# Four of the eight blocks of two feed-forward column groups as seven products of two by two blocks, with the sums formed in float32

## The chip, the cores and the metric

The kernel runs on one core of one Trainium2 chip. The metric is the device time of one execution, in microseconds (us). The core has a matmul engine (TensorE, in the profile PE with its weight loads PEld), a vector engine (DVE), a scalar engine (ACT), GpSimd (POOL) and a queue that starts transfers (SP). Matmuls write to eight PSUM banks of 128 x 512 float32; DVE and ACT read the banks, POOL does not.

## The reference, cut to what matters

Two layers of a decoder trunk on 256 tokens of width 1024, each with three gated token mixers and a feed-forward part. The change is in the feed-forward part of each layer:

```python
h2 = _rms_norm(x, ffn_norm)
x = x + (jax.nn.silu(h2 @ w_ffn_gate) * (h2 @ w_ffn_up)) @ w_ffn_down
```

Here h2 is 256 x 1024 and gate and up are 1024 x 2816 each. All is float32 and has to come out at float32's accuracy or close to it.

## The kernel before, in words

**Products.** TensorE multiplies numbers of a shorter format (F32R). So every operand is split in two, `hi` (rounded by ACT, `hi_of`, L223) and `lo` (what is left, a subtraction on DVE, `lo_of`, L226), and a product is three matmuls: hi by hi, hi by lo, lo by hi.

**Weights.** `weight_plan` (L51) cuts every weight into pieces of 128 x 1024 numbers at most, in the order of their use; for the feed-forward's first layer a piece is two blocks of 128 rows of the contraction by 512 columns. `dma_piece` (L241) loads a piece on SP's queue into one of five `raw` tiles. `split_piece` (L268) splits it into one of five pairs `whi`, `wlo` and then starts the load of the piece that takes the freed raw tile. `take` (L277) is called for each piece that is to be multiplied; it first splits the piece three further on.

**First layer of the feed-forward.** `ffn` (L1002) goes over the columns in groups of 1024: 512 of gate, then the same 512 of up, five such groups and a last one of half the size, for both layers. Gate and up take one `rows_job` (L297) each. It has one bank for each half of the 256 rows (b = 0, 1) and goes over the eight contraction blocks k in four pieces; for each k and each b it issues three matmuls with 512 columns, so 12 for a piece, 48 for a job and 96 for a group. The inputs are the normalised rows, `xs[k]`, as hi and lo:

```python
self.mm(ps[b], h, wh, k == 0, False)
self.mm(ps[b], h, wl, False, False)
self.mm(ps[b], lo, wh, False, k == nk - 1)
```

After gate's job ACT takes tanh of each bank (L1008) and DVE forms the gate from it (L1009); after up's job DVE multiplies it in (`product`, L1012). The rows so made are transposed by TensorE (`transposed`, L465, eight matmuls for a group), and split for the second layer, in `hidden_pairs` (L994), which is called after the second piece of the next group.

**Before it.** `out_proj` (L975) ends the mixers. It adds its two halves of columns to the rows x (`x_tm`, L989), and in its second half it calls `norm_pairs((0, 1))` (L473): TensorE transposes the first half of x into a bank, ACT writes gain times the bank as hi (L224) and DVE what is left as lo (L231). Pairs 2 and 3 follow in the feed-forward's first job. ACT also squares x for the norm (L413).

**Order.** The kernel is written as a stream of operations in program order. The framework then sets a fixed order for each engine, by its own estimate of when an operation is ready, and adds the waits; so an operation may stand ahead of one that was written before it. PSUM is two rings of four banks, `bank` for weight products and `att` for transposes and attention. `fr` is a ring of 18 pairs of tiles for split operands, `f` one of nine float32 tiles.

Of the kernel before, what the change touches and what calls it, by code (L numbers as in the profile page):

```python
# [12 lines left out]
F32 = mybir.dt.float32  # L13
# [35 lines left out]


def weight_plan():  # L51
    plan = []

    def block(name, l, nk, c0, ncols):
        per = max(1, PIECE // ncols)
        for k in range(0, nk, per):
            plan.append((name, l, k, min(per, nk - k), c0, ncols))

    def mixer_in(l, off):
        for c in range(0, 1024, 256):  # L60
            block("w_in", l, KT, off + c, 256)

    for l in range(DEPTH):
        block("w_in", l, KT, OFF_C, N_C)
        mixer_in(l, OFF_AQ)
        block("mla_w_uq", l, 3, 0, 768)
        block("mla_w_ukv", l, 2, 0, 1024)
        block("w_in", l, KT, OFF_AV, 512)
        mixer_in(l, OFF_BQ)
# [7 lines left out]
        for n in range(2 * FF // 512):  # L77
            block("w_ffn", l, KT, n * 512, 512)
# [5 lines left out]
    return plan  # L84


BRANCHES = ((0, "w_branch_a"), (2, "w_branch_c"), (1, "w_branch_b"))
PLAN = weight_plan()


def shape_constants():
# [84 lines left out]
def fields(t):  # L176
    v = t.rearrange("p (c f t) -> p c f t", c=2, f=2)
    return v[:, :, 0], v[:, :, 1]
# [6 lines left out]
class Build:  # L185
    def __init__(self, nc, tc, ctx, x, xt, w, lam, fnorm, cst, out):
        self.nc, self.tc = nc, tc
        self.x_in, self.xt_in, self.w_in = x, xt, w
        self.lam_in, self.fnorm_in, self.cst_in, self.out = lam, fnorm, cst, out
        self.cp = cp = ctx.enter_context(tc.tile_pool(name="cp", bufs=1))  # L190
        pp = ctx.enter_context(tc.tile_pool(name="pp", bufs=1, space=PSUM))

        def ring(n, cols, dt, name, pool=cp):
            return Ring([pool.tile([128, cols], dt, name=f"{name}{i}") for i in range(n)])

        self.banks = ring(N_DENSE, 512, F32, "bank", pp)
# [7 lines left out]
        self.raw = [cp.tile([128, PIECE], F32, name=f"raw{i}") for i in range(N_RAW)]  # L204
# [31 lines left out]
    def split(self, hi, lo, src, scale=None):  # L236
        self.hi_of(hi, src, 1.0 if scale is None else scale)
        self.lo_of(lo, src, hi, scale)


    def dma_piece(self, queue=None):  # L241
        if self.n_dma < len(PLAN):
# [3 lines left out]
            (queue or self.nc.sync).dma_start(out=self.raw[self.n_dma % N_RAW][:, :n], in_=src)  # L246
            self.woff += 128 * n
            self.n_dma += 1

    def first_split(self):  # L250

        hi, lo, raw = self.whi[0], self.wlo[0], self.raw[0]
# [10 lines left out]
        self.n_split = 1  # L263
        self.dma_piece()
        self.xg.append(t)
        self.xs += chunks([t])

    def split_piece(self):  # L268
        i = self.n_split
        if i < len(PLAN):  # L270
            n = PLAN[i][3] * PLAN[i][5]
            j = i % N_PIECE
            self.split(self.whi[j][:, :n], self.wlo[j][:, :n], self.raw[i % N_RAW][:, :n])
            self.n_split += 1
            self.dma_piece()

    def take(self):  # L277
        self.split_piece()
        i = self.taken
        self.taken += 1  # L280
        _, _, _, nk, _, nc_ = PLAN[i]
# [29 lines left out]
    def setup(self):  # L311
# [10 lines left out]
        for p in range(1, 4):  # L322
            nc.sync.dma_start(out=self.x0[p], in_=self.x_in[:, G_W + 512 * p:G_W + 512 * p + 512])
            self.dma_piece()
        self.ones = cp.tile([128, 128], F32, name="ones")
        nc.vector.memset(self.ones, 1.0)  # L326
        self.ones_r = cp.tile([128, 128], F32R, name="ones_r")
# [11 lines left out]
        self.vc = [cp.tile([128, 8, 2, 64], F32R, name=f"vc{b}") for b in range(2)]  # L339
        self.q_tm = cp.tile([128, 2, 8, 96], F32, name="q_tm")  # L340
        self.k_tm = cp.tile([128, 2, 8, 96], F32, name="k_tm")
# [131 lines left out]
    def norm_pairs(self, pairs, g0):  # L473
        for p in pairs:
            bank, ps = self.transposed(self.x_tm, p * 256)
            self.split_pair(p, ps, g0)
            self.att.put(bank)


    def dense(self, l):  # L480
# [491 lines left out]
            pump(2 if s < SLOW else 1)  # L972


    def out_proj(self, pairs, nk, g0, late):  # L975
        self.fresh_norm()
        self.ss = [self.small(), self.small()]
        for n in range(2):
            bank = [self.banks.get() for _ in range(2)]
            for i, _ in enumerate(self.rows_job(bank, ChunkList(pairs), nk)):  # L980
                if n == 0 and i == 0:
                    late()
                if n == 1 and i == 1:
                    self.norm_pairs((0, 1), g0)
# [17 lines left out]
    def ffn(self):  # L1002
# [8 lines left out]
        def product(b, a, u):  # L1011
            nc.vector.scalar_tensor_tensor(out=a, in0=a, scalar=self.rr[:, b:b + 1], in1=u, op0=ALU.mult, op1=ALU.mult)  # L1012

        for i in range(5):
            a = [self.f.get() for _ in range(2)]
            bank = [self.banks.get() for _ in range(2)]
            for j, _ in enumerate(self.rows_job(bank, self.xs, KT)):
                yield
                if j == 1 and self.waiting:
                    self.hidden_pairs(*self.waiting)  # L1020
            for b in range(2):
                gated(b, a[b], bank[b])
            self.banks.put(*bank)
# [84 lines left out]
    def run(self):  # L1108
        self.n_norm = 0
        self.setup()  # L1110
        for l in range(DEPTH):
# [30 lines left out]
            self.attention(l, pump)  # L1142
            for _ in stream:
                pass
            self.out_proj(self.mp, KT, G_FFN + 8 * l, lambda: self.mixed(1))
            stream = self.ffn()
            pump(1)
            self.norm_pairs((2, 3), G_FFN + 8 * l)
# [6 lines left out]
        assert self.taken == len(PLAN)  # L1155


def pack_weights(arrs):
# [40 lines left out]
```

## Time and profile before

| | |
|---|---|
| Time, median of 3 runs | 880.74 us (880.54 to 880.96) |
| Profiled execution, its own time | 880.81 us |
| Its span, first to last instruction | 879.0 us |
| PE busy, and PEld | 871.7 us (99%), 755.8 us (86%) |
| DVE busy | 591.7 us (67%) |
| ACT busy | 503.0 us (57%) |
| POOL busy | 55.5 us (6%) |
| DMA | 155.90 MB, mean 177 GB/s |

Busy is the share of the span in which an engine had an instruction under way. Matmuls are pipelined, so PE's busy time overlaps from one matmul to the next, and the mean duration of one is longer than the step from one to the next.

### The profile page before, as it was taken

What the parts mean: (1) busy time and instruction counts of PE and PEld (TensorE: products, weight loads), DVE (VectorE), ACT (ScalarE), POOL (GpSimd) and SP (SyncE); (2) the same over time, 40 slices, a digit from 0 to 9 for tenths busy, and PEclk for the clock granted to TensorE, in tenths of its full rate; (3) what the DMA queues carried; (4) which work ended last, traced back from release to release, by engine and by line L of the source; (5) the groups of instructions that cost most, each with busy time, mean ns of one, the idle gap of its engine ahead of it and who ended that gap; (6) DMA issues with size and microseconds to landing.
All of it is one profiled execution on the core that took longest, in us unless ns stands there. A gap on an engine that the chain in (4) does not pass through costs nothing.

```text
span 879.0 us, 12626 instructions
## 1 busy us (share of the span) xinstructions
PE 871.7 (99%) x4656; PEld 755.8 (86%) x4656; DVE 591.7 (67%) x1000; ACT 503.0 (57%) x854; POOL 55.5 (6%) x83
## 2 busy tenths in 40 slices
PE   9999999999999999999999999999999999999997
PEld 9999988888888888888899899888888888888886
DVE  6988878765666665555467888787556666566544
ACT  7896777544455444444376867675454644444432
POOL 1430310000000000000011303000000000000000
PEclk9999999999999999999999999999999999999999
DMA  9756444456656566656475553444555456655541
GB/s 350 256 168 198 136 148 144 145 177 192 183 169 208 177 187 187 186 179 191 127 227 174 168 171 130 150 143 163 178 187 185 169 192 204 203 175 186 190 144 48
DMA packets 45134, 155.90 MB, mean 177 GB/s; under 512 B 5008, under 2 KB 6032, under 8 KB 45072
## 3 DMA queue, kind: packets, MB, share of 16 engines
q1 hardware_dynamic: 44640, 154.36, 55.2%
q8 instruction: 36, 0.59, 0.3%
q10 hardware_dynamic: 432, 0.74, 0.2%
q14 instruction: 26, 0.21, 0.1%
HBM read 154.03 MB, written 1.05 MB: 176 GB/s over the span
## 4 chain that ended last, share of the span: by engine, by line
PE 99%; DVE 0%; POOLq 0%; issue 0%; DVEq 0%
PE bank L211 89%; PE att L211 6%; PE att L470 2%; PE att L755 1%; PE att L803 0%; PE att L805 0%; PE att L804 0%; PE att L729 0%; PE att L887 0%; POOLq L1194 0%; DVE x_tm L1100 0%; DVE x_tm L1081 0%; DVE f L1083 0%; DVEq L1194 0%; DVE ones L326 0%
## 5 line engine op out<-in xcount | busy, mean ns | idle before, releaser
L211 PE MATMUL bank<-whi,fr 128*128 128x512 f32 (+1 forms) x2032 | 632.8, 389 | 0.0
L229 DVE TENSOR_TENSOR wlo<-raw,whi 128x1024 fp32r<-128x1024 f32 (+3 forms) x295 | 353.3, 1200 | 246.7 <-ACT whi L224 245.8
L224 ACT ACTIVATE whi<-raw 128x1024 fp32r<-128x1024 f32 (+3 forms) x295 | 305.2, 1038 | 304.9 <-PE bank L211 268.6
L211 PEld LDWEIGHTS bank<-whi,fr 128*128 128x128 f32 x2032 | 379.5, 188 | 72.6
L211 PE MATMUL bank<-wlo,fr 128*128 128x512 f32 (+1 forms) x1016 | 390.9, 387 | 0.0
L211 PEld LDWEIGHTS bank<-wlo,fr 128*128 128x128 f32 x1016 | 190.7, 188 | 36.4 <-DVE wlo L229 0.3
L211 PE MATMUL bank<-fr,whi 128*128 128x256 f32 x512 | 95.0, 285 | 0.0
L211 PEld LDWEIGHTS bank<-fr,whi 128*128 128x128 f32 x512 | 80.1, 191 | 0.2
L211 PE MATMUL bank<-fr,wlo 128*128 128x256 f32 x256 | 72.7, 284 | 0.0
L211 PEld LDWEIGHTS bank<-fr,wlo 128*128 128x128 f32 x256 | 49.0, 191 | 0.0
L795 ACT ACTIVATE s<-s,small 128x256 f32<-128x256 f32 (+1 forms) x80 | 35.9, 456 | 2.6 <-DVE small L793 2.2
L394 POOL TENSOR_TENSOR r<-small,mhalf 128x2 f32<-128x2 f32 x4 | 2.8, 709 | 477.8 <-DVE small L420 463.7
L224 ACT ACTIVATE fr<-att 128x512 fp32r<-128x512 f32 (+2 forms) x54 | 28.4, 561 | 6.5 <-PE att L211 3.5
L229 DVE TENSOR_TENSOR fr<-att,fr 128x512 fp32r<-128x512 f32 (+2 forms) x46 | 28.2, 636 | 1.9 <-ACT fr L224 1.8
L394 POOL TENSOR_TENSOR small<-small,mhalf 128x2 f32<-128x2 f32 (+1 forms) x12 | 10.3, 856 | 283.7 <-DVE small L1090 177.5
L211 PE MATMUL att<-fr,fr 96*128 96x256 f32 (+3 forms) x152 | 26.1, 277 | 0.0
L224 ACT ACTIVATE fr<-f 64x512 fp32r<-64x512 f32 (+2 forms) x40 | 23.3, 582 | 3.0 <-DVE f L947 1.1
L211 PEld LDWEIGHTS att<-fr,fr 96*128 96x128 f32 (+1 forms) x152 | 22.6, 190 | 0.6
L1008 ACT ACTIVATE f<-bank,rh 128x512 f32<-128x512 f32 (+1 forms) x24 | 15.6, 654 | 12.2 <-PE bank L211 12.2
L651 ACT ACTIVATE f<-bank,rh 128x512 f32<-128x512 f32 x24 | 16.4, 689 | 9.8 <-PE bank L211 9.7
L211 PE MATMUL att<-whi,fr 128*128 128x288 f32 (+1 forms) x72 | 19.9, 293 | 0.0
L1009 DVE SCALAR_TENSOR_TENSOR f<-f,bank 128x512 f32<-128x512 f32 (+1 forms) x24 | 15.4, 644 | 4.9 <-ACT f L1008 4.9
(139 smaller groups left out, 606.8 us busy)
## 6 DMA issues: line engine op xcount, KB each, us to landing
raw<-w SPq DMA_DIRECT2D x272, 512.0 KB, 3.6
raw<-w SPq DMA_DIRECT2D x15, 336.0 KB, 2.9
raw<-w SPq DMA_DIRECT2D x6, 384.0 KB, 3.2
x_tm<-xt SPq DMA_DIRECT2D x2, 512.0 KB, 6.5
f<-x SPq DMA_DIRECT2D x3, 256.0 KB, 5.7
out<-x_tm SPq DMA_DIRECT2D x2, 320.0 KB, 2.4
f<-fnorm SPq DMA_DIRECT2D x2, 256.0 KB, 4.1
out<-x_tm ACTq DMA_DIRECT2D x2, 192.0 KB, 2.2
```

Source lines behind the costliest of these rows:

```text
L211: self.nc.tensor.matmul(out, lhsT, rhs, start=start, stop=stop, skip_group_check=True)
L224: self.nc.scalar.activation(out=hi, in_=src, func=AF.Copy, scale=scale)
L229: self.nc.vector.tensor_tensor(out=lo, in0=src, in1=h, op=ALU.subtract)
L394: self.nc.gpsimd.tensor_tensor(out=out, in0=v, in1=self.mhalf[:, 0:v.shape[1]], op=ALU.pow)
L470: self.nc.tensor.transpose(ps[:, c, b * 128:b * 128 + 128], src[b][:, c0 + c * 128:c0 + c * 128 + 128], self.ident)
L651: nc.scalar.activation(out=t[b], in_=bank[b], func=AF.Tanh, scale=self.rh[:, b:b + 1])
L755: nc.tensor.transpose(ps[0:96, c, b * 128:b * 128 + 128], src[:, b, 2 * p + c, :], self.ident)
L795: nc.scalar.activation(out=s[:, SL[b]], in_=s[:, SL[b]], func=AF.Exp, bias=mn[:, b:b + 1], scale=-1.0, accum_out=z[:, b:b + 1])
L1008: nc.scalar.activation(out=a, in_=g, func=AF.Tanh, scale=self.rh[:, b:b + 1])
L1009: nc.vector.scalar_tensor_tensor(out=a, in0=a, scalar=1.0, in1=g, op0=ALU.add, op1=ALU.mult)
```

## The change

Rows 0 to 127 and 128 to 255 of the input (r0, r1), and blocks 0, 1 and 2, 3 of the contraction (h0, h1), give four quarters of 128 x 256; gate and up columns and the same two halves of the contraction give four weight blocks b11, b12, b21, b22, each one piece. In groups 1 and 3 of the five (`FAST`), in both layers, the product of these is done as seven block products in place of eight, in the Winograd order of Strassen's scheme. The input's four sums S1 to S4 are formed once for each layer, on POOL (`combined_inputs`), and split; the weights' sums T are formed by DVE in the raw tiles, four subtractions of 128 x 1024 for a group (`differences`), and then split like a piece. Blocks 4 to 7 are multiplied as before. A group is now 11 pieces, of 6 or 12 matmuls, 90 in all. It has four banks, of which `a` and `c` are read in the middle of their accumulation: by ACT into float32 tiles (three copies), to which DVE adds later banks (four additions).

Around it: one ring of eight banks in place of two of four; seven raw tiles, held until a piece's last use, in place of five; 17 `fr` pairs in place of 18; `q_tm` and `k_tm` in one tile and `vc` in another, whose space the sums use; and pairs 0 and 1 of the feed-forward's input are first written by ACT as float32 (`keep`) and then split, so that the sums can be formed from them.

```diff
-N_PAIR = 18
+N_PAIR = 17
-N_DENSE = 4
-N_RAW = 5
+N_RAW = 7
+FAST = (1, 3)
...
+    def fast(name, l, c1, c2):
+        b11, b12, b22, b21 = (load(name, l, k, 2, c, 512) for k, c in ((0, c1), (0, c2), (2, c2), (2, c1)))
+        rest = [load(name, l, k, 2, c, 512) for c in (c2, c1) for k in (4, 6)]
...
+        split(b12, before=[(b12, b12, b11)], after=[(b12, b22, b12)])
+        split(b11, after=[(b11, b12, b11)])
+        split(rest[0], frees=(rest[0],))
+        split(b12, after=[(b12, b21, b12)])
+        split(rest[1], frees=(rest[1],))
+        split(b11, frees=(b11,))
+        split(b21, frees=(b21,))
+        split(b22, frees=(b22,))
+        split(b12, frees=(b12,))
+        for i in rest[2:]:
+            split(i, frees=(i,), pool=POOL_LOW)
...
-        self.banks = ring(N_DENSE, 512, F32, "bank", pp)
-        self.att = ring(8 - N_DENSE, 512, F32, "att", pp)
+        self.banks = self.att = ring(8, 512, F32, "bank", pp)
...
+    def differences(self, ops):
+        for out, a, b in ops:
+            self.nc.vector.tensor_tensor(out=self.raw_of[out], in0=self.raw_of[a], in1=self.raw_of[b], op=ALU.subtract)
+
     def split_piece(self):
...
+            self.differences(before)
+            hi, lo, raw = self.whi[j][:, :n], self.wlo[j][:, :n], self.raw_of[at][:, :n]
+            self.hi_of(hi, raw)
+            (self.lo_pool if pool else self.lo_of)(lo, raw, hi)
+            self.differences(after)
             self.n_split += 1
-            self.dma_piece()
+            for f in frees:
+                self.raw.put(self.raw_of.pop(f))
+                self.dma_piece()
...
+            if keep:
+                x = self.f.get()
+                for c in range(2):
+                    self.hi_of(x[:, c * 256:c * 256 + 256], ps[:, c], self.gains[:, g0 + 2 * p + c:g0 + 2 * p + c + 1])
+                t = self.fr.pair()
+                self.split(*fields(t), split_rows(x))
...
+    def combined_inputs(self):
...
+        for out, a, b, op in ((s1, quarter(1, 0), quarter(1, 1), ALU.add), (s2, s1, quarter(0, 0), ALU.subtract),
+                              (s3, quarter(0, 0), quarter(1, 0), ALU.subtract), (s4, quarter(0, 1), s2, ALU.subtract)):
+            nc.gpsimd.tensor_tensor(out=out, in0=a, in1=b, op=op)
...
+            self.split(hi, lo, t)
...
+    def fast_job(self, evac):
...
+        order = [[("c", s1)], [("a", x(0, 0))], [("c", x(0, 4)), ("d", x(1, 4))], [("a", s2)], [("c", x(0, 6)), ("d", x(1, 6))],
+                 [("a", s3)], [("b", x(0, 2))], [("c", s4)], [("a", x(1, 2))],
+                 [("b", x(0, 4)), ("a", x(1, 4))], [("b", x(0, 6)), ("a", x(1, 6))]]
...
+                    for a, w in ((hi, wh), (hi, wl), (lo, wh)):
+                        self.mm(bank[n], a, w, n not in begun, False)
...
+            evac(i, bank)
...
+            def evac(i, bank):
+                if i == 0:
+                    nc.scalar.activation(out=u1, in_=bank["c"], func=AF.Copy)
+                elif i == 1:
+                    nc.scalar.activation(out=g0, in_=bank["a"], func=AF.Copy)
+                elif i == 3:
+                    nc.scalar.activation(out=u0, in_=bank["a"], func=AF.Copy)
+                elif i == 4:
+                    nc.vector.tensor_tensor(out=u1, in0=u1, in1=bank["d"], op=ALU.add)
+                elif i == 5:
+                    nc.vector.tensor_tensor(out=u1, in0=u1, in1=bank["a"], op=ALU.add)
+                elif i == 7:
+                    nc.vector.tensor_tensor(out=u0, in0=u0, in1=bank["c"], op=ALU.add)
+                elif i == 10:
+                    nc.vector.tensor_tensor(out=g0, in0=g0, in1=bank["b"], op=ALU.add)
+                    for b, (g, u) in enumerate(((g0, u0), (bank["a"], u1))):
+                        gated(b, a[b], g)
+                        product(b, a[b], u)
...
+        for _ in range(N_RAW - 5):
             self.dma_piece()
```

## Rows read from the trace of the kernel before

**Rows 1.** the page, part 1: busy us of each engine (share of span), instructions

```profile
PE 871.7 (99%) x4656; PEld 755.8 (86%) x4656; DVE 591.7 (67%) x1000; ACT 503.0 (57%) x854; POOL 55.5 (6%) x83
```

**Rows 2.** the page, part 4: chain that ended last, by engine

```profile
PE 99%; DVE 0%; POOLq 0%; issue 0%; DVEq 0%
```

**Rows 3.** stretches: length, busy time (instructions) by engine, granted clock, DMA

```profile
core 0: us, PE busy (x) PEld busy (x) DVE busy (x) ACT busy (x) POOL busy (x), PEclk, DMA share, GB/s
0.00:22.00 22.00, 20.94 (x131) 20.36 (x132) 13.48 (x30) 16.09 (x31) 3.28 (x11) 1.00 0.93 350
257.00:386.00 129.00, 129.00 (x593) 107.18 (x592) 79.07 (x87) 61.70 (x71) 0.59 (x1) 1.00 0.62 188
304.60:327.25 22.65, 22.65 (x105) 18.84 (x105) 13.70 (x14) 10.71 (x13) 0.00 (x0) 1.00 0.63 186
692.00:820.00 128.00, 128.00 (x586) 106.39 (x586) 75.72 (x82) 58.88 (x67) 0.00 (x0) 1.00 0.58 189
```

**Rows 4.** chain of waits in the feed-forward: start, length, what

```profile
304.60 21.78 PE bank L211 x96
326.38 0.87 PE att L470 x8
```

**Rows 5.** timeline of DVE there: start, length, operation, [idle before, releaser]

```profile
304.85 1.23 DVE L229 TENSOR_TENSOR wlo<-raw,whi 128x1024 fp32r<-128x1024 f32 x1 [1.50 <-ACT whi L224]
306.00 1.29 DVE L229 TENSOR_TENSOR fr<-att,fr 128x512 fp32r<-128x512 f32 x2
...
310.13 1.37 DVE L1009 SCALAR_TENSOR_TENSOR f<-f,bank 128x512 f32<-128x512 f32 x2 [0.44 <-ACT f L1008]
...
320.48 1.40 DVE L1012 SCALAR_TENSOR_TENSOR f<-f,rr,bank 128x512 f32<-128x512 f32 x2
```

**Rows 6.** timeline of ACT there

```profile
301.04 1.06 ACT L224 ACTIVATE whi<-raw 128x1024 fp32r<-128x1024 f32 x1 [1.66 <-PE bank L211]
...
304.72 1.07 ACT L224 ACTIVATE fr<-att 128x512 fp32r<-128x512 f32 x2
...
309.41 1.37 ACT L1008 ACTIVATE f<-bank,rh 128x512 f32<-128x512 f32 x2 [0.98 <-PE bank L211]
310.68 1.05 ACT L224 ACTIVATE whi<-raw 128x1024 fp32r<-128x1024 f32 x1
```

**Rows 7.** timeline of PE where the feed-forward begins

```profile
251.80 0.82 PE L470 MATMUL att<-ident,x_tm 128*128 128x128 f32 x6
252.38 0.48 PE L211 MATMUL bank<-whi,fr 128*128 128x512 f32 x1
...
252.86 0.50 PE L211 MATMUL bank<-whi,fr 128*128 128x512 f32 x1
...
253.66 0.40 PE L211 MATMUL bank<-wlo,fr 128*128 128x512 f32 x1
253.89 0.82 PE L470 MATMUL att<-ident,x_tm 128*128 128x128 f32 x6
```

**Rows 8.** timeline of ACT, same stretch

```profile
252.33 0.84 ACT L224 ACTIVATE fr<-att,first 128x256 fp32r<-128x256 f32 x2 [1.95 <-PE att L470]
253.06 0.63 ACT L413 ACTIVATE f<-x_tm 128x512 f32<-128x512 f32 x1
```

**Rows 9.** timeline of DVE, same stretch

```profile
246.29 1.28 DVE L989 TENSOR_TENSOR x_tm<-x_tm,bank 128x512 f32<-128x512 f32 x2
...
252.90 0.69 DVE L989 TENSOR_TENSOR x_tm<-x_tm,bank 128x512 f32<-128x512 f32 x1 [0.66 <-PE bank L211]
```

**Rows 10.** groups by shape: count, busy us, mean ns, idle before

```profile
L224 ACT ACTIVATE fr<-f 128x512 fp32r<-128x512 f32 x8 | 4.9, 618 | 0.0
...
L989 DVE TENSOR_TENSOR x_tm<-x_tm,bank 128x512 f32<-128x512 f32 x12 | 7.9, 683 | 1.7 <-PE bank L211 1.7
...
L638 POOL TENSOR_TENSOR f<-q_tm,cs 128x256 f32<-128x256 f32 x4 | 4.0, 989 | 29.9 <-ACT q_tm L599 29.9
```

**Rows 11.** DMA issues: count, KB each, median us to landing

```profile
raw<-w SPq DMA_DIRECT2D x272, 512.0 KB, 3.6
```

More of the change, by code (lines that the diff above doesn't have):

```diff
@@ L51, in weight_plan, with load @@
 def weight_plan():
-    plan = []
+    plan, splits = [], []
+    def load(*piece):
+        plan.append(piece)
+        return len(plan) - 1
     def block(name, l, nk, c0, ncols):
@@ L56, in block, with split @@
         for k in range(0, nk, per):
-            plan.append((name, l, k, min(per, nk - k), c0, ncols))
+            i = load(name, l, k, min(per, nk - k), c0, ncols)
+            splits.append((i, (), (), (i,), False))
+    def fast(name, l, c1, c2):
+        b11, b12, b22, b21 = (load(name, l, k, 2, c, 512) for k, c in ((0, c1), (0, c2), (2, c2), (2, c1)))
+        rest = [load(name, l, k, 2, c, 512) for c in (c2, c1) for k in (4, 6)]
+        def split(i, before=(), after=(), frees=(), pool=False):
+            splits.append((i, before, after, frees, pool))
+        split(b12, before=[(b12, b12, b11)], after=[(b12, b22, b12)])
[9 more added lines that the diff above has]
+            split(i, frees=(i,), pool=POOL_LOW)
     def mixer_in(l, off):
@@ L76, in weight_plan @@
             block("w_out", l, KT, n * 512, 512)
-        for n in range(2 * FF // 512):
-            block("w_ffn", l, KT, n * 512, 512)
+        for i in range(5):
+            if i in FAST:
+                fast("w_ffn", l, i * 1024, i * 1024 + 512)
+            else:
+                block("w_ffn", l, KT, i * 1024, 512)
+                block("w_ffn", l, KT, i * 1024 + 512, 512)
+        block("w_ffn", l, KT, 5120, 512)
         if l + 1 < DEPTH:
@@ L83, in weight_plan @@
             block("w_ffn_down", l, NF, 0, 1024)
-    return plan
+    return plan, splits
 BRANCHES = ((0, "w_branch_a"), (2, "w_branch_c"), (1, "w_branch_b"))
-PLAN = weight_plan()
+PLAN, SPLITS = weight_plan()
 def shape_constants():
@@ L203, in __init__ @@
         self.row = ring(1, 256, F32, "row")
-        self.raw = [cp.tile([128, PIECE], F32, name=f"raw{i}") for i in range(N_RAW)]
+        self.qk = cp.tile([128, 3 * PIECE], F32, name="qk")
+        self.raw = Ring([cp.tile([128, PIECE], F32, name=f"raw{i}") for i in range(N_RAW)])
+        self.raw_of = {}
         self.whi = [cp.tile([128, PIECE], F32R, name=f"whi{i}") for i in range(N_PIECE)]
@@ L241, in dma_piece @@
     def dma_piece(self, queue=None):
-        if self.n_dma < len(PLAN):
+        if self.n_dma < len(PLAN) and self.raw.free_tiles:
             _, _, _, nk, _, ncols = PLAN[self.n_dma]
@@ L245, in dma_piece @@
             src = self.w_in[self.woff:self.woff + 128 * n].rearrange("(p n) -> p n", p=128)
-            (queue or self.nc.sync).dma_start(out=self.raw[self.n_dma % N_RAW][:, :n], in_=src)
+            t = self.raw_of[self.n_dma] = self.raw.get()
+            (queue or self.nc.sync).dma_start(out=t[:, :n], in_=src)
             self.woff += 128 * n
@@ L266, in first_split @@
         self.xs += chunks([t])
+    def differences(self, ops):
+        for out, a, b in ops:
+            self.nc.vector.tensor_tensor(out=self.raw_of[out], in0=self.raw_of[a], in1=self.raw_of[b], op=ALU.subtract)
     def split_piece(self):
         i = self.n_split
-        if i < len(PLAN):
-            n = PLAN[i][3] * PLAN[i][5]
+        if i < len(SPLITS):
+            at, before, after, frees, pool = SPLITS[i]
+            n = PLAN[at][3] * PLAN[at][5]
             j = i % N_PIECE
-            self.split(self.whi[j][:, :n], self.wlo[j][:, :n], self.raw[i % N_RAW][:, :n])
+            self.differences(before)
[3 more added lines that the diff above has]
+            self.differences(after)
             self.n_split += 1
-            self.dma_piece()
+            for f in frees:
+                self.raw.put(self.raw_of.pop(f))
+                self.dma_piece()
     def take(self):
@@ L471, in transposed, with norm_pairs @@
         return bank, ps
-    def norm_pairs(self, pairs, g0):
+    def norm_pairs(self, pairs, g0, keep=False):
         for p in pairs:
             bank, ps = self.transposed(self.x_tm, p * 256)
-            self.split_pair(p, ps, g0)
-            self.att.put(bank)
+            if keep:
[4 more added lines that the diff above has]
+                self.split(*fields(t), split_rows(x))
+                self.xg.append(t)
+                self.xs += chunks([t])
+                self.xkept.append(x)
+            else:
+                self.split_pair(p, ps, g0)
+            self.att.put(bank)
@@ new lines, in combined_inputs, with quarter @@
+    def combined_inputs(self):
+        nc = self.nc
+        def quarter(rows, half):
+            return split_rows(self.xkept[half])[:, :, rows * 128:rows * 128 + 128]
+        s = [self.qk[:, i * 256:i * 256 + 256] for i in range(4)]
+        s1, s2, s3, s4 = (split_rows(t) for t in s)
+        for out, a, b, op in ((s1, quarter(1, 0), quarter(1, 1), ALU.add), (s2, s1, quarter(0, 0), ALU.subtract),
+                              (s3, quarter(0, 0), quarter(1, 0), ALU.subtract), (s4, quarter(0, 1), s2, ALU.subtract)):
+            nc.gpsimd.tensor_tensor(out=out, in0=a, in1=b, op=op)
+        self.f.put(*self.xkept)
+        self.sums = []
+        for i, t in enumerate(s):
+            hi, lo = (self.vcs[:, o:o + 256] for o in (512 * i, 512 * i + 256))
+            self.split(hi, lo, t)
+            self.sums.append([(hi[:, k * 128:k * 128 + 128], lo[:, k * 128:k * 128 + 128]) for k in range(2)])
@@ new lines, in fast_job, with x @@
+    def fast_job(self, evac):
+        def x(rows, k0):
+            return [tuple(self.xs[k0 + k][:, o + rows * 128:o + rows * 128 + 128] for o in (0, 256)) for k in range(2)]
+        s1, s2, s3, s4 = self.sums
+        bank = {n: self.banks.get() for n in "abcd"}
+        order = [[("c", s1)], [("a", x(0, 0))], [("c", x(0, 4)), ("d", x(1, 4))], [("a", s2)], [("c", x(0, 6)), ("d", x(1, 6))],
+                 [("a", s3)], [("b", x(0, 2))], [("c", s4)], [("a", x(1, 2))],
+                 [("b", x(0, 4)), ("a", x(1, 4))], [("b", x(0, 6)), ("a", x(1, 6))]]
+        begun = set()
+        for i, targets in enumerate(order):
+            for k, (wh, wl) in enumerate(self.take()):
+                for n, lhs in targets:
+                    hi, lo = lhs[k]
+                    for a, w in ((hi, wh), (hi, wl), (lo, wh)):
+                        self.mm(bank[n], a, w, n not in begun, False)
+                        begun.add(n)
+            evac(i, bank)
+            yield i
+        self.banks.put(*bank.values())
@@ L972, in attention, with out_proj @@
             pump(2 if s < SLOW else 1)
-    def out_proj(self, pairs, nk, g0, late):
+    def out_proj(self, pairs, nk, g0, late, keep=False):
         self.fresh_norm()
+        self.xkept = []
         self.ss = [self.small(), self.small()]
@@ L983, in out_proj @@
                 if n == 1 and i == 1:
-                    self.norm_pairs((0, 1), g0)
+                    self.norm_pairs((0, 1), g0, keep)
             if n == 1:
@@ L1012, in product, with fast @@
             nc.vector.scalar_tensor_tensor(out=a, in0=a, scalar=self.rr[:, b:b + 1], in1=u, op0=ALU.mult, op1=ALU.mult)
+        def fast():
+            a = [self.f.get() for _ in range(2)]
+            g0, u0, u1 = (self.f.get() for _ in range(3))
+            def evac(i, bank):
[16 more added lines that the diff above has]
+                        product(b, a[b], u)
+                    self.f.put(g0, u0, u1)
+            for i in self.fast_job(evac):
+                yield
+                if i == 3 and self.waiting:
+                    self.hidden_pairs(*self.waiting)
+            self.waiting = (a, 512)
         for i in range(5):
+            if i in FAST:
+                yield from fast()
+                continue
             a = [self.f.get() for _ in range(2)]
@@ L1020, in ffn @@
                     self.hidden_pairs(*self.waiting)
+            if i == 0:
+                self.combined_inputs()
             for b in range(2):
@@ L1154, in run @@
                 self.out_proj(self.hp, NF, G_ATT + 8 * (l + 1), lambda: self.hidden_pairs(*self.waiting))
-        assert self.taken == len(PLAN)
+        assert self.taken == len(SPLITS) and self.n_dma == len(PLAN)
 def pack_weights(arrs):
```

15 lines of the change are left out of this document (9 added, 6 removed).

## The prediction

> **What bounds the kernel now.** I read the page first. PE has matmuls under way in 99% of the span, and the chain of waits that ended last is PE for 99% [rows 1, 2]. Busy time alone would not prove that PE never waits, since its matmuls overlap, so I went on to the chain inside the feed-forward: 96 matmuls of one group in 21.78 us, then eight transposes in 0.87 us, then the next 96 [rows 4]. That is 0.2269 us from one matmul to the next, and it holds from group to group with nothing between. DVE is busy for 13.7 and ACT for 10.7 of such a group's 22.65 us, and the granted clock is 1.00, the 2.4 GHz level, in every stretch I looked at [rows 3]. So in the feed-forward only the number of matmuls and their step count, as long as DVE and ACT keep ahead. They keep ahead by far: ACT starts a hi as soon as its slot of five is free (its idle time ends on PE) and with 1.06 us for hi and 1.23 us for lo a piece is ready some 2.4 us later, while PE comes to it four pieces, 10.9 us, after the slot came free [rows 5, 6]. About 8 us are spare.
>
> **What it removes.** A changed group has 90 matmuls in place of 96 (seven block products of six matmuls and four pieces of twelve). At 0.2269 us that is 1.36 us for each group, 22.65 to 21.29 us, and over two groups in two layers 24 matmuls, **5.45 us** [rows 4]. They all lie on the chain.
>
> **What it adds to DVE.** Eleven lo's in place of eight and four subtractions of the same shape, 15 at 1.23 us, four additions from a bank (nearest row 0.683 us), and as before gate, product and transposed rows (1.37, 1.40, 1.29 us): 25.2 us, in place of 13.9, in a group that lasts 21.3 us on PE [rows 5, 10]. **So DVE owes 4 us in each changed group.** ACT gets 11 hi's at 1.06, three copies at 0.69 (the tanh row), and as before 1.37 and 1.07: 16.2 us, which fits [rows 6].
>
> Does the debt reach PE? I wrote the group down as a ledger from these durations: a piece is split when its slot is free and DVE is, a bank is read when its matmuls are done, of two that are ready the earlier in the program goes first. A read of a bank starts 0.29 us after the next matmul could have (a last matmul that starts at 252.38 plus one step, against DVE at 252.90) [rows 7, 9]. In us from the group's start, PE begins pieces 1 to 11 at 0, 1.36, 2.72, 5.45, 7.68, 10.40, 11.76, 13.12, 14.48, 15.85 and 18.57; their lo's end at -6.9, -4.4, -2.0, -0.1, 3.8, 5.0, 6.4, 8.1, 11.2, 13.1 and 15.1. The least spare time is 2.7 us, at the tenth piece; the 8 us ahead at the start pay the debt, and the normal group behind it, where DVE has 8.7 us over, refills the lead. I take **0**. Done again with 1.40 us for 1.23 the ledger still loses only 0.3 us in a layer, with 1.45 it loses 1.9, with 1.50 4.0.
>
> **Waits inside a group.** Banks c and a are read in the middle of their sums. The tightest is c: piece 1 ends at 1.36, ACT copies from 1.65 to 2.34, and c's next matmuls may start at 2.72, so 0.38 us are spare. The other is a: DVE adds it from 13.13 to 13.82, its next matmul is at 14.48. In the forecast both fit, **0**. If ACT does a hi before that copy (both are released by the same matmul), c is 0.68 us late, and PE stands with all that is queued behind; if DVE does one more lo before that addition, a is 0.57 us late. That bounds this term by 0 and 1.25 us a group.
>
> **Where the feed-forward begins.** Now ACT writes hi of pair 0 in two halves at once from the bank, the first ready about 0.48 us after 252.33, and PE's first feed-forward matmul follows at 252.86 [rows 7, 8]. With `keep` ACT writes both halves as float32 (0.84 us), and then hi in one operation of 512 (0.618 us, [rows 10]): ready at 253.8, 1.0 us later. PE has one thing to fill in, the six transposes of 253.89, which need DVE's addition that ends at 253.59 [rows 7, 9]. Done first they end near 254.35, and the four matmuls that before had been done by then (252.86 to 253.66) come after: four times 0.227, **0.9 us for each layer, 1.8 in all**. The lower end is 0: the rows for pair 0 are complete at 247.57, well before the transposes are issued, so the order could bring these forward [rows 9]. The upper end is 1.75 us a layer: 0.98 us plus the square, 0.63 us and its accumulator's read, if ACT does it in between [rows 8]. I take 0.9, by the rows as they stand.
>
> **At nothing.** The four input sums are a chain on POOL of four operations, about 0.99 us each by the nearest row, and four small splits; they can start with pairs 0 and 1 and are first needed a whole group, 22 us, later. Without that cover they would cost 4 us a layer and the small splits behind them [rows 3, 10]. Loads: the number is unchanged, the last piece of a group is started after its third split and used at the eleventh, against 3.6 us to land; without the cover a late load costs those 3.6 [rows 11]. At the start two more weight loads stand on SP's queue ahead of the identity and the rows for the first norm: 0.69 MB at the 350 GB/s of that stretch is 2.0 us later for these; PE has weight products for that time, whose banks are now eight; between -1.06 us (all of PE's idle time there) and 2.0, I take 0 [rows 3]. The common ring, 17 `fr` pairs and the merged tiles let the order change in the attention; PE has no idle time to win there, and a bank late by one piece would cost 2.7 us; I take 0.
>
> **Sum.** 880.81 (the profiled execution; its span is 879.0) - 5.45 + 1.8 = 877.16. The runs' median is 0.07 lower, so **877.1 us**.
>
> **Rivals.** *The start is free*: the transposes of pairs 0 and 1 move up to where their rows are ready, or the scheduler finds other work. 880.74 - 5.45 = 875.3. For it speaks the 3.6 us between 247.57 and the transposes; against it that they had that time before and weren't moved.
>
> *Reads in the middle of a sum hold PE*: the copy of c comes behind a hi, 0.68 us in four groups, 2.7 us: 879.8; with the addition of a late as well, 882.1. For it: ACT's spare time at c is 0.38 us, less than any of its operations. Against it: tanh stood ahead of the next hi where both were near (309.41, 310.68) [rows 6]. The Trainium skill ("PSUM — Partial Sum Buffer", section "PSUM bank collisions raise a hardware error") says that two engines' accesses to one bank and quadrant must be kept apart, reads as well as writes; by that rule each such read is a full stop for the bank's next matmul, and the time would go towards this rival. No row of before has a read amid a sum, so the trace does not say.
>
> *DVE sets the pace* (the other side): if the fixed order spends the lead before a changed group, or puts lo's behind additions that wait for PE, the group lasts as long as DVE's work, 25.2 us in place of 21.3. In full that is 3.95 us in four groups, 892.9; half of it, since normal groups lie between, 885.0. It makes the kernel slower from 1.35 us a group on ((1.76 + 3.65) / 4), or, by the ledger, from some 1.48 us for each operation of 1.23. For it: 118% of DVE in those groups, where before it was 60%, and an order that was made from estimates. Against it: the ledger's 2.7 us.
>
> **How the numbers follow.** What a measurement of this kernel can tell from no change is about 0.2%, 1.76 us. Forecast, 876.2 to 879.0: 0.53. Free start, 874.9 to 876.2: 0.15. Held by reads, or the like elsewhere, 879.0 to 882.5: 0.17. DVE, above 882.5: 0.15. So faster 0.68, the same 0.17, slower 0.15. The range from 874.9 to 882.4 leaves out a little over 0.15.
>
> **What would show it.** PE's matmuls fall from 4656 to 4632. In the chain a changed group reads 90 matmuls in 20.4 us, in one piece; a break at the third piece means the copy of c, one at the ninth the addition of a, at pieces 5 to 10 with PE released by DVE the slow rival. DVE's busy time rises by some 45 us for the four groups and by a few us for the sums, ACT's by about 25. At the feed-forward's start the first matmul comes about 1 us later after the transposes. The forecast is wrong if the step of the matmuls in pieces of six is not 0.227 us, or if PE gets new idle time outside the feed-forward.

## The result, and the profile after

The changed kernel takes **888.33 us** (887.93 to 889.72, four runs), against 880.83 in the same runs for the kernel before: 1.0088 times its time, 95% interval 1.0071 to 1.0106. So it is slower by 7.5 us where 3.6 us less were forecast, an error of 11 us. The profiled execution took 888.32 us, with a span of 886.5.

First the page of the changed kernel, part 1 (as [rows 1]) and the chain by engine (as [rows 2]):

```profile
PE 870.9 (98%) x4632; PEld 751.0 (85%) x4632; DVE 631.2 (71%) x1048; ACT 524.6 (59%) x890; POOL 62.5 (7%) x91
...
PE 94%; DVE 4%; issue 1%; ACT 1%; POOLq 0%; POOL 0%; DVEq 0%; ACTq 0%
```

The 24 matmuls are gone (4656 to 4632), and DVE has 39.5 us more. But 6% of the chain is no longer PE's. Which waits these are, the list of PE's waits says: line and tile that waited, who ended the wait, us in total, times, longest. Before, it had one row (1.0 us, on the ones at the very start). After, its longest are:

```profile
PE bank L245 <- ACT fr L258: 3.0, 2, 1.5
PE bank L245 <- DVE pt L263: 2.0, 2, 1.0
PE bank L519 <- DVE x_tm L1090: 1.1, 2, 0.6
PE bank L245 <- DVE ones L375: 1.0, 1, 1.0
PE bank L245 <- ACT pt L258: 0.8, 1, 0.8
PE bank L245 <- DVE fr L263: 0.5, 2, 0.3
```

`fr` and `x_tm` are the feed-forward's start, once in each layer; `pt` is attention. Inside the changed groups there is no wait. The chain in the feed-forward of layer 0 (start, length, what; as [rows 4]):

```profile
257.11 0.73 ACT f L258 x2
257.84 0.95 ACT whi L258
258.79 0.02 issue
258.82 1.47 DVE wlo L263
260.29 0.16 issue
260.45 1.23 DVE fr L263
261.68 0.04 issue
261.73 24.41 PE bank L245 x106
...
288.86 32.98 PE bank L245 x145
```

From 261.73 on it is PE alone. In the stretch from 288.86, which holds most of the first changed group, it takes 32.98 / 145 = 0.2274 us a matmul, almost as dense as before (0.2269). Nearly all that is lost, is lost ahead of 261.73. There PE (as [rows 7]) stands three times:

```profile
256.97 0.87 PE L519 MATMUL bank<-ident,x_tm 128*128 128x128 f32 x6 [0.56 <-DVE x_tm L1090]
259.36 0.50 PE L245 MATMUL bank<-whi,fr 128*128 128x512 f32 x1 [1.51 <-ACT fr L258]
...
261.73 0.96 PE L245 MATMUL bank<-whi,fr 128*128 128x512 f32 x3 [0.27 <-DVE fr L263]
```

ACT shows why (as [rows 8]). Between the float32 copy of pair 0 (255.66) and the hi that is made from it (258.66) it does the square, the float32 copy of pair 1 and a weight's hi:

```profile
255.66 0.84 ACT L258 ACTIVATE f<-bank,first 128x256 f32<-128x256 f32 x2 [1.95 <-PE bank L519]
256.39 0.63 ACT L462 ACTIVATE f<-x_tm 128x512 f32<-128x512 f32 x1
256.91 0.20 ACT L462 ACTIVATION_READ_ACCUMULATOR f<-x_tm 128x1 f32 x1
257.00 0.84 ACT L258 ACTIVATE f<-bank,first 128x256 f32<-128x256 f32 x2
257.72 1.07 ACT L258 ACTIVATE whi<-raw 128x1024 fp32r<-128x1024 f32 x1
258.66 0.64 ACT L258 ACTIVATE fr<-f 128x512 fp32r<-128x512 f32 x1
```

In DVE's rows there (as [rows 9]) the same operations that take 1.23 [rows 5] and 0.68 us elsewhere take 1.71 and 1.22:

```profile
258.82 1.71 DVE L263 TENSOR_TENSOR wlo<-raw,whi 128x1024 fp32r<-128x1024 f32 x1 [1.90 <-ACT whi L258]
260.45 1.22 DVE L263 TENSOR_TENSOR fr<-f,fr 128x512 fp32r<-128x512 f32 x1
...
262.86 0.68 DVE L263 TENSOR_TENSOR fr<-f,fr 128x512 fp32r<-128x512 f32 x1
```

They lie beside the input sums, which the fixed order puts here and not behind them:

```profile
258.72 0.72 POOL L549 TENSOR_TENSOR qk<-qk,f 128x256 f32<-128x256 f32 x1
259.52 1.60 POOL L549 TENSOR_TENSOR qk<-f,qk 128x256 f32<-128x256 f32 x1
```

**By stages.** I took the start of the first transpose of `x_tm` in each `norm_pairs`, and the last matmul, in both traces. Such marks cut each execution in four, and the differences add up. In us against the kernel before, for the changed kernel and for the experiments to come (all from their profiled executions):

| kernel | layer 0 to its feed-forward | feed-forward 0 | layer 1 to its feed-forward | feed-forward 1 | sum |
|---|---|---|---|---|---|
| changed | +3.33 | +0.73 | +2.68 | +0.75 | +7.50 |
| e1, start undone | +3.07 | -2.29 | +2.67 | -2.28 | +1.18 |
| e2, two rings | +2.78 | +1.78 | +0.10 | +0.74 | +5.40 |
| e3, both | +2.84 | -2.28 | +0.10 | -2.29 | -1.63 |
| e4, before with one ring | +3.06 | -0.01 | +3.19 | +0.01 | +6.24 |
| e5, e3 and late load calls | +2.51 | -2.31 | +0.10 | -2.31 | -2.00 |
| e6, e5 with three groups | +2.45 | -2.23 | +0.10 | -2.26 | -1.94 |
| e7, no sums | +2.79 | +0.21 | +2.72 | +0.20 | +5.92 |
| e8, e3 and late tiles | +0.42 | -2.31 | +0.10 | -2.31 | -4.10 |
| e9, e8 with one ring | +3.05 | -2.29 | +2.68 | -2.27 | +1.17 |

So 6.0 of the 7.5 us were lost in the mixers, where the change multiplies nothing else; and each feed-forward lost 0.74 in place of winning 2.72, so 3.46 went there, nearly all of it at its start. (From e8 it will be seen that 0.41 of the 3.46 lie in the changed groups; the start is the other 3.05.)

What happens in the mixers is a change of the fixed order. The transposes of attention's last scores (PE, line of `p_transposed`; before, then after) come 22.7 us earlier:

```profile
171.43 0.29 PE L803 MATMUL att<-ident,s 128*128 128x128 f32 x1
```

```profile
148.75 0.30 PE L903 MATMUL bank<-ident,s 128*128 128x128 f32 x1
```

In the other kernels with one ring (e1, e4, e9) they start near 148 us too, in those with two rings (e2, e3, e8) at 167 to 172. With the one ring of eight banks the fixed order runs attention ahead and leaves weight products for later. Before, weight products stood between the steps of attention; now PE comes to the next step of attention while ACT is still splitting its input. After, at such a place:

```profile
87.09 0.27 PE L905 MATMUL bank<-ident,s 128*128 128x128 f32 x1
88.16 0.36 PE L245 MATMUL bank<-fr,fr 96*128 96x256 f32 x1 [0.79 <-ACT pt L258]
```

In the kernel before PE has nothing but weight products from 86.2 to 89.4 us, and no gap.

### The profile page after: what moved, and what is told of

Read it like the earlier page. It is cut to its first block, busy times and chain, and to the rows that moved or that the text cites. A ratio compares the mean times of both kernels' runs of the same rounds, so it can differ in the third digit from the quotient of the medians.

```text
span 886.5 us, 12660 instructions
## 1 busy us (share of the span) xinstructions
PE 870.9 (98%) x4632; PEld 751.0 (85%) x4632; DVE 631.2 (71%) x1048; ACT 524.6 (59%) x890; POOL 62.5 (7%) x91
## 4 chain that ended last, share of the span: by engine, by line
PE 94%; DVE 4%; issue 1%; ACT 1%; POOLq 0%; POOL 0%; DVEq 0%; ACTq 0%
PE bank L245 90%; PE bank L519 2%; DVE wlo L263 1%; PE bank L855 1%; DVE fr L263 0%; DVE s L893 0%; PE bank L903 0%; PE bank L904 0%; PE bank L905 0%; DVE fr L265 0%; PE bank L829 0%; ACT f L258 0%; ACT whi L258 0%; DVE pt L263 0%; DVE s L891 0%
## 5 line engine op out<-in xcount | busy, mean ns | idle before, releaser
L245 PE MATMUL bank<-whi,fr 128*128 128x512 f32 (+2 forms) x2024 | 614.8, 385 | 3.6 <-ACT fr L258 3.0
L263 DVE TENSOR_TENSOR wlo<-raw,whi 128x1024 fp32r<-128x1024 f32 (+3 forms) x307 | 367.6, 1203 | 214.8 <-ACT whi L258 213.0
L258 ACT ACTIVATE whi<-raw 128x1024 fp32r<-128x1024 f32 (+3 forms) x307 | 317.6, 1038 | 282.0 <-PE bank L245 248.8
L245 PE MATMUL bank<-wlo,fr 128*128 128x512 f32 (+2 forms) x1012 | 380.0, 384 | 0.0
L258 ACT ACTIVATE fr<-bank 128x512 fp32r<-128x512 f32 (+2 forms) x54 | 28.5, 559 | 8.2 <-PE bank L519 4.8
L263 DVE TENSOR_TENSOR fr<-bank,fr 128x512 fp32r<-128x512 f32 (+2 forms) x46 | 28.1, 635 | 1.7 <-ACT fr L258 1.7
L245 PE MATMUL bank<-fr,fr 96*128 96x256 f32 (+3 forms) x152 | 26.4, 275 | 1.1 <-ACT pt L258 0.8
L245 PEld LDWEIGHTS bank<-fr,fr 96*128 96x128 f32 (+1 forms) x152 | 23.2, 190 | 2.5 <-ACT pt L258 1.0
L245 PE MATMUL bank<-whi,vcs 128*128 128x512 f32 x64 | 22.7, 400 | 0.0
L306 DVE TENSOR_TENSOR raw<-raw,raw 128x1024 f32<-128x1024 f32 x16 | 19.5, 1221 | 2.1 <-DMA raw<-w 1.9
```

Source lines behind the costliest of these rows:

```text
L245: self.nc.tensor.matmul(out, lhsT, rhs, start=start, stop=stop, skip_group_check=True)
L258: self.nc.scalar.activation(out=hi, in_=src, func=AF.Copy, scale=scale)
L263: self.nc.vector.tensor_tensor(out=lo, in0=src, in1=h, op=ALU.subtract)
L306: self.nc.vector.tensor_tensor(out=self.raw_of[out], in0=self.raw_of[a], in1=self.raw_of[b], op=ALU.subtract)
```

## The experiments

Times are medians against 880.9 to 881.0 us for the kernel before in the same runs; short diffs against the kernel named.

**e1, the start undone.** Against the changed kernel: hi and lo of pairs 0 and 1 straight from the bank, the float32 copy beside them.

```diff
             if keep:
+                self.split_pair(p, ps, g0)
                 x = self.f.get()
...
-                t = self.fr.pair()
-                self.split(*fields(t), split_rows(x))
-                self.xg.append(t)
-                self.xs += chunks([t])
...
```

> Changed kernel, but pairs 0 and 1 of the feed-forward's input are split straight from the bank as before, and ACT writes their float32 copies after that. Theory (the start of the feed-forward is lost by the order on ACT: hi of pair 0 stands behind both pairs' copies, a square and a weight's hi): its first matmul comes some 3 us earlier in each layer, so 888.3 - 6 = 882.3, between 881.3 and 883.3. Rival (what is lost there is DVE, slowed beside POOL's sums): POOL's sums stay, so at most 0.7 us in each layer comes back, 887 to 888.

Measured: 882.22 us, ratio 1.0013 (1.0004 to 1.0021), 6.1 us less than the changed kernel. The feed-forwards go from +0.74 to -2.29 each, the mixers stay. The two waits on `fr` and the wait on `x_tm` are gone from PE's list. So the loss there was the detour through float32, with what ACT did in between.

**e2, two rings.** Against the changed kernel: four banks each; a and b of a changed group from `att`, c and d from `bank`.

```diff
-        self.banks = self.att = ring(8, 512, F32, "bank", pp)
+        self.banks = ring(4, 512, F32, "bank", pp)
+        self.att = ring(4, 512, F32, "att", pp)
...
```

> Changed kernel with two rings of four banks again; a changed group takes a and b from one, c and d from the other. Theory (the common ring lets the fixed order run attention ahead, and PE then waits in it, 3.3 us in layer 0 and 2.65 us in layer 1): 888.3 - 5.9 = 882.4, between 881 and 883.5, with the attention's stalls of 0.3 to 1.3 us gone. Rival (17 pairs, the merged tiles or seven raw tiles do it): 887.5 to 889.

Measured: 886.37 us, 1.0056 (1.0043 to 1.0068): 2.0 us less, not 5.9. Layer 1's mixers are back (+0.10), layer 0's are not (+2.78), so something else holds layer 0. That layer 0's feed-forward is a further 1.0 us longer comes from the clock and not from the rings: in this profiled execution the granted clock was 0.50, the 1.2 GHz level, for 3.41 us from 259.36 on, after PE had stood for 0.56 and 1.51 us (columns as in [rows 3]):

```profile
259.36:262.77 3.41, 3.41 (x9) 2.67 (x8) 3.41 (x8) 3.20 (x9) 2.04 (x2) 0.50 0.45 151
```

Its matmuls start 0.42 to 0.43 us apart there. The profile of the changed kernel has the same stops, with the clock at 1.00. The one run of e2 with the changed kernel's mean clock (0.998; the others have 0.996 and 0.997) took 885.04 us, 3.3 less than the changed kernel.

**e3, both.**

> Both edits, the start and the two rings. If the two losses are separate places they add: 888.3 - 6 - 5.9 = 876.4, between 875 and 878, that is the kernel before less 24 matmuls (875.4) and some 1 us. If one of the two theories falls, 882; if both, 887 to 888.

Measured: 879.51 us, 0.9982 (0.9973 to 0.9991): less than before, but 4.0 above 875.5, the kernel before less 24 matmuls. PE's waits beyond the one on the ones are now two, in layer 0's latent stage (the part of the mixers ahead of attention, where its q and k are formed):

```profile
60.70 0.31 PE L852 MATMUL att<-ident,qk 128*96 128x128 f32 x1 [0.33 <-ACT qk L721]
62.23 0.53 PE L852 MATMUL att<-ident,qk 128*96 128x128 f32 x3 [1.21 <-POOL qk L738]
```

**e4, the ring alone.** The kernel before with nothing of the change but one ring of eight.

```diff
-        self.banks = ring(N_DENSE, 512, F32, "bank", pp)
-        self.att = ring(8 - N_DENSE, 512, F32, "att", pp)
+        self.banks = self.att = ring(8, 512, F32, "bank", pp)
```

> Kernel before, with the one ring of eight banks and nothing else. Theory (the ring alone costs the attention): 880.8 + 5.9 = 886.7, between 884 and 888. Rival (the ring is innocent): 880.3 to 881.3.

Measured: 887.34 us, 1.007 (1.0058 to 1.0083), 6.3 us slower: 3.06 in layer 0's mixers, 3.19 in layer 1's, nothing in the feed-forwards.

**e5, the two load calls later.** Against e3: in its start the kernel issues two more weight loads ahead of the identity, the rows and the tables.

```diff
-        for _ in range(N_RAW - 5):
-            self.dma_piece()
...
                 self.lambdas()
+                for _ in range(N_RAW - 5):
+                    self.dma_piece()
```

> The kernel with both corrections (pairs 0 and 1 split straight from the bank; two rings of four banks), and the two extra weight loads of the setup issued after the loads of tables() and lambdas() instead of ahead of ident and x_tm. Theory: what was left over (879.5 measured, 875.5 by the sum) is the 2.8 us of layer 0's latent stage, where PE waited 1.21 us for a POOL rope product and 0.33 us for an ACT copy because x_tm, ident and the tables came 2 to 5 us later on SP's queue. Moved behind them, the loads cost nothing: 879.5 - 2.8 = 876.7 us (875.8 to 877.6), and the two waits are gone from PE's list. Rival: the waits come from the merged tile of q_tm and k_tm and from 17 pairs instead of 18, and stay: 879.2 to 879.8 us.

Measured: 879.28 us, no different from 879.51. It didn't do what it was to do: with seven empty tiles the next loads are free to go at once, and the order takes them ahead of `x_tm`. SP's queue (start and length of the issue) in the kernel before, then in e5:

```profile
7.25 0.33 SPq L457 DMA_DIRECT2D x_tm<-xt  x1
```

```profile
6.57 2.71 SPq L282 DMA_DIRECT2D raw<-w  x4
9.79 0.33 SPq L505 DMA_DIRECT2D x_tm<-xt  x1
```

**e6, three changed groups in a row.** Against e5.

```diff
-FAST = (1, 3)
+FAST = (1, 2, 3)
```

> The previous kernel (late loads, both corrections) with three changed groups that follow one another, 1, 2 and 3, instead of 1 and 3. Theory: VectorE owes 25.2 us per changed group of 21.3 us on TensorE, and only the ordinary group between two changed ones pays that back; with three in a row the same ledger that gave no loss for (1, 3) leaves TensorE idle 6.0 us per layer, against 12 matmuls more saved (12 x 0.2269 = 2.72 us over both layers, 1.36 per layer): +4.6 us per layer, that is about 9.3 us above the previous kernel, 884 to 888 us if it is at 876.7, and the waits of PE on DVE in the third group. Rival: the DVE debt does not reach TensorE, as it did not for two groups: another 2.7 us less, about 874 us.

Measured: 879.45 us, equal to e5, so neither theory holds. The 1.36 us of the third group are lost again in each layer, but not by DVE. At the start of the third group the order puts bank a's next product only one matmul behind its first one, and PE waits until ACT has copied the bank. The rows are PE's, then ACT's:

```profile
325.56 0.39 PE L246 MATMUL bank<-whi,fr 128*128 128x512 f32 x1
326.41 0.50 PE L246 MATMUL att<-whi,vcs 128*128 128x512 f32 x1 [0.46 <-ACT f L1118]
```

```profile
325.76 0.60 ACT L1118 ACTIVATE f<-att 128x512 f32<-128x512 f32 x1 [1.64 <-PE att L246]
```

From start to start that is 0.85 us where 0.23 is the step, so 0.62 us lost; the place where the second changed group begins loses 0.27, and the step behind each is 0.1 longer: 1.1 us in all. In the second group the copy comes behind a hi and a tanh (ACT, from 301.82 on; the copy at 303.38), much as the rival of the reads had it. In the third ACT isn't late, it had been idle for 1.64 us, and PE's own order makes the stop. The DVE debt doesn't reach PE. In the third group DVE even waits for ACT, and its rows say one thing that the ledger had wrong:

```profile
332.20 4.62 DVE L264 TENSOR_TENSOR wlo<-raw,whi 128x1024 fp32r<-128x1024 f32 x4
...
342.44 1.23 DVE L264 TENSOR_TENSOR wlo<-raw,whi 128x1024 fp32r<-128x1024 f32 x1 [0.96 <-ACT whi L259]
```

Four lo's in a row take 4.62 us, 1.155 each: the 1.22 us of one overlap the next. Over the three groups, 282.2 to 349.5 us, DVE is busy for 63.9 of 67.3 us, but the work of three groups isn't all in it: it has their number of lo's, 33, and only 8 of the 12 subtractions. What a changed group costs DVE is read from the pages: 655.6 us busy in e6 against 636.2 in e5, so 9.7 for each of the two added groups on top of the 13.7 of an ordinary one [rows 3]. That is 23.4 us in place of the ledger's 25.2, a debt of about 2 us to TensorE in place of 4, and DVE's lead pays it.

**e7, no sums.** Against the changed kernel.

```diff
-        for out, a, b, op in ((s1, quarter(1, 0), quarter(1, 1), ALU.add), ...
-            nc.gpsimd.tensor_tensor(out=out, in0=a, in1=b, op=op)
+        s = [quarter(rows, half) for half in range(2) for rows in range(2)]
...
```

> The changed kernel as it was timed (888.3 us), without the four sums on POOL: their splits read the quarters of the float32 copy in place of the sums, so the changed groups multiply other data. It tells how much of the 3.45 us per layer at the start of the feed-forward is the order of ACT's work and how much is that two-input DVE instructions ran longer beside POOL's (wlo 1.71 us for 1.23, fr lo 1.22 for 0.68). Theory: the order of ACT's work alone sets when TensorE starts; without the sums only the 0.27 us wait for the second fr lo goes: 888.3 - 2 x 0.3 = 887.7 us (887.2 to 888.3). Rival: the lengthened DVE instructions hold TensorE, 1.0 us per layer: 886.3 us (885.5 to 887). Either way the two DVE rows should be back at 1.23 and 0.68 us.

Measured: 887.23 us (in other runs than the changed kernel's 888.33). The first FFN matmul still waits 1.5 us for ACT, as the theory had it. The DVE rows are back:

```profile
258.27 1.22 DVE L263 TENSOR_TENSOR wlo<-raw,whi 128x1024 fp32r<-128x1024 f32 x1 [1.90 <-ACT whi L258]
259.42 0.68 DVE L263 TENSOR_TENSOR fr<-f,fr 128x512 fp32r<-128x512 f32 x1
```

and each feed-forward is 0.53 us shorter: between the 0.3 of the theory and the 1.0 of its rival. So the sums' overlap was 0.5 of the start's 3.05 us, and ACT's order and detour the rest. The further 0.5 us in layer 0's mixers (+2.79 for +3.33) I can't explain by the sums; four runs of e7 at the same mean clock (0.998) lie 1.0 us apart, 886.54 to 887.53, so it is within their scatter.

**e8, late tiles.** Against e5: the ring of raw tiles has five until layer 0's attention; then the other two join, tied to a value of the latent stage so that no load goes early.

```diff
...
+            if l == 0:
+                for t in self.raw_late:
+                    self.nc.gpsimd.tensor_copy(t[:, 0:32], self.kpe[:, 0])
+                    self.raw.put(t)
+                    self.dma_piece()
             self.attention(l, pump)
```

> Both corrections again, and now the two added raw tiles join the ring only before layer 0's attention, behind a copy of 128 x 32 on POOL that needs a value of the latent stage. Moving only the two load calls had changed nothing (879.28): the loads still came ahead of x_tm on SP's queue, since an empty tile makes a load free to go early. With five tiles until then SP's queue is as it was before. Theory: the early loads change the fixed order of layer 0's latent stage (one q_tm copy of ACT at 57.6 us in place of 53.4, a 1.2 us wait of PE on the rope product of POOL); with them gone that stage costs what it did before, 879.3 - 2.6 = 876.7 us (875.8 to 877.4), and both waits leave PE's list. Rival: the merged tiles of q and k or the 17 pairs make it: 879.0 to 879.7 us.

Measured: **877.11 us**, 0.9955 (0.9940 to 0.9969), less than either kernel takes. Layer 0's mixers go from +2.51 to +0.42, and PE's list of waits has only the ones again. On SP's queue the first `x_tm` goes out at 7.25 us, as in the kernel before. What had changed shows in one ACT copy of layer 0's latent stage, which the order puts back to its place. In e3, then in e8, where its start is as in the kernel before (53.44):

```profile
57.89 0.57 ACT L696 ACTIVATE qk<-bank,rq 128x384 f32<-128x384 f32 x1
```

```profile
53.65 0.58 ACT L695 ACTIVATE qk<-bank,rq 128x384 f32<-128x384 f32 x1
```

The merged tiles and the 17 pairs are still in e8, so they don't make the loss. Whether the loads ahead of `x_tm` do, or that the order had seven tiles so early, e8 doesn't tell: it takes both away.

Each feed-forward of e8 wins 2.31 us, not 2.72. The 0.41 isn't at the start: from the first transpose of `x_tm` to the first feed-forward matmul PE takes 1.51 us (251.76 to 253.27), before 1.52. It is in the changed groups, for the most part in products with the tile that holds the split sums (`vcs`):

```profile
287.77 0.39 PE L247 MATMUL bank<-whi,vcs 128*128 128x512 f32 x1
...
290.56 0.39 PE L247 MATMUL att<-whi,fr 128*128 128x512 f32 x1
...
293.51 0.39 PE L247 MATMUL bank<-wlo,fr 128*128 128x512 f32 x1
```

From 287.77 twelve matmuls with `vcs` take 2.79 us, a step of 0.233; from 290.56 thirteen with `fr` take 2.95, a step of 0.227. The 48 such matmuls of a feed-forward make some 0.3 us. In e7, where the tile holds no sums, its step is 0.233 too; why, no run shows.

**e9, late tiles and one ring.** Against e8, the ring of the change.

> As the kernel before it in this list, but with the one ring of eight banks of the change. It tells how the ring's cost and the early loads' cost stand together. Theory: both spoil the order of the same stage, layer 0's, so they do not add: without the early loads the ring alone costs what it cost in the kernel before, 6.3 us, which makes 876.7 + 6.3 = 883.0 us (881.8 to 884.0), no better than the 882.2 us of the kernel that has the ring and the early loads. Rival: the two add up; the ring costs the 2.7 us that lay between the kernels with one and two rings (882.2 and 879.5), which makes 879.4 us (878.5 to 880.3).

Measured: 881.84 us, 1.001 (1.0001 to 1.0019), 4.7 above e8. Layer 0's mixers are again at +3.05, as with the ring alone (+3.06) or with ring and loads (+3.07). So the two costs don't add: either one loses layer 0's 2.5 to 3 us, and only the ring loses layer 1's.

## Why the prediction was wrong, step by step

Three terms failed. The start was put at 0.9 us a layer and cost 3.05; the common ring and the early loads were put at nothing, and cost 6.3 us (e4) and 2.2 to 2.4 us (e5 and e3 against e8).

- **Removed, 5.45 us: right, but for a step.** 24 matmuls are gone. In e8 each feed-forward is 2.31 us shorter, which is 2.72 less 0.41 in the changed groups, where products with `vcs` go at 0.233 us and not at 0.227. That was one of the prediction's signs of being wrong, and so was new idle time of PE outside the feed-forward: 3.7 us more in the mixers.
- **DVE's debt, 0: right in result, wrong in size.** No wait of PE lies in the changed groups. The ledger was on the safe side: it came to 4 us of debt a group where e6 against e5 shows about 2, in part since it took an operation's duration (1.23 us) for the step to the next (1.155).
- **Reads in the middle of a sum, 0: right here.** ACT's copy of c ran from 283.42 to 284.02, before the 1.36 us of bank a's product had ended; PE didn't stop. The Trainium skill ("PSUM — Partial Sum Buffer", section "PSUM bank collisions raise a hardware error") wants two engines' accesses to one bank kept apart, reads as well as writes. The trace agrees: here the reads fall where PE writes another bank, and it shows no stop; in e6, where bank a's next product stands right behind the read, PE waits 0.46 us.
- **The start, 0.9 us a layer: the size failed, 3.05 measured.** I counted ACT's two steps in place of one, and bounded the term by the square in between, 1.75. I didn't ask what else becomes ready for ACT in that gap: the copy of pair 1 and a weight's hi also went between. And I had the sums hidden behind a group of 22 us, when the order put them at once, beside the two DVE operations that PE waited for. That these ran longer there (1.71 for 1.23, 1.22 for 0.68) e7 shows. The Trainium skill ("SBUF — State Buffer", section "Who interferes with whom") says that a DVE instruction with two SBUF inputs contends with a GpSimd instruction that reads SBUF; the trace agrees, at 0.5 us a layer. With the bank split directly, as in e8, the start costs nothing.
- **One ring of eight, 0: failed, 6.3 us alone (e4).** "PE has no idle time to win there" was true and the wrong question. With the larger ring the order goes ahead with attention (148.75 for 171.43), as I take it since it waits for fewer banks there; and where the rows show PE waiting (87.09 to 88.16), it had no weight product between two steps of attention. My other price, a bank late by one piece, was never the way it would cost.
- **Loads at the start, 0: failed, 2.2 to 2.4 us (e5 and e3 against e8).** I weighed 2.0 us of delay against PE's cover at the start, and there it was covered. The cost came 50 us later, as another order of the latent stage (the ACT copy at 57.89 for 53.65).
- **Rivals.** None came true. The slow side that I gave a chance, DVE's pace, was the wrong one: the time fell where I had put that rival (above 882.5, at 0.15), but by luck. The change is slower by 7.5 us through the order outside its groups and at the feed-forward's start.

With the three terms undone (e8) the kernel takes 877.11 us. That this is the sum that I had is luck in part: the sum has 1.8 us for a detour that e8 doesn't make, and e8 has 0.8 us in the changed groups and 0.5 in the mixers that the sum hasn't. The price of the products was sound, the zeros were not. Since layer 0's two costs overlap, the parts of the 11 us aren't a plain sum. From the other end, e8 plus ring (4.7) is 881.8, and the start's other 3.05 us in each layer make 887.9, against 888.3; the early loads add only what is left, as e1 against e9 (882.2, 881.8) shows.

What stays open: which operation's estimate tips the order of layer 0's latent stage, and why products with `vcs` take a longer step.

## What to carry to other kernels

Where a framework orders the engines, a buffer count is a change of order: any ring made larger, and any load made free to go early, must be priced at every stage that uses the ring or the queue, even if nothing waits there now. Try such edits by themselves on the kernel before (e4 needed one line), and when an intermediate step is put in front of the first operand of a stage, ask what else becomes ready for that engine in between. A tile count isn't undone by moving the calls that use it (e5); tie the new tile to a late value (e8).

## What the runs showed of the hardware

Beside POOL's two-input operations, DVE's lo of 128 x 1024 took 1.71 us for 1.23 and that of 128 x 512 1.22 for 0.68; without them (e7) both were back. A POOL operation was longer as well: among the four sums, of one shape, three took 0.73 us and the one beside both lo's 1.60. Back to back, DVE's operations of 1.22 us follow each other at 1.155 us. Two stops of PE, of 0.56 and 1.51 us, were followed in e2 by 3.41 us at the 1.2 GHz level, and in the profile of the changed kernel by none.
